# A two-layer transformer trunk: paired softmax reciprocals, one modulation row on TensorE, and the residual weighted ahead of the output projection

## The chip, the cores and the metric

The kernel runs on one core of one Trainium2 chip. The core has TensorE (PE; its weight loads are listed apart as PEld), VectorE (DVE), ScalarE (ACT), GpSimd (POOL) and SyncE (SP), which here only issues DMAs. The metric is the device time of one execution in microseconds (us), as the median of several runs. The profile is that of one execution.

## The reference

Two layers act on 1024 tokens of width 1024, in float32. In short:

```python
mod = silu(c) @ w_ada[l] + b_ada[l]
shift, scale, gate = split(mod, 3)
h = x * (1 + scale) + shift
# one projection h @ w_in feeds three groups of heads and a gate:
#   6 latent heads (MLA, rotary part, RMS-normed latents), causal softmax
#   6 dilated heads: three dilated windows mixed by their softmax sums, ALiBi
#   4 sparse heads: an indexer scores all keys, the best 256 are attended, ALiBi
y = concat(latent, dilated, sparse) * silu(p_gate)
x = layer_norm(ALPHA * x + (1 + gate) * (y @ w_out[l]), ln_g[l], ln_b[l])
```

`ALPHA` is the fourth root of 4. `c` is one row of 1024 values, so `mod` is a product of one row with a 1024 x 3072 matrix.

## The kernel before

All tensors are cut into tiles of 128 partitions. Products keep float32 accuracy by splitting each operand into a rounded part `hi` and a rest `lo` and adding three products (`three`). For a weight, `split_w` (L188) loads a raw tile on SP, ScalarE makes `hi` (L192) and by default GpSimd makes `lo = raw - hi` (L193). The modulated input is held as eight blocks `HA[k]`, one for each 128 columns of the model width, each with a `hi` and a `lo` tile of 128 x 1024.

**The order of the work.** The program is written in a plain order, but a planner orders it at build time: it simulates the engines with its own cost estimates and puts instructions of different heads, stages and layers beside each other wherever their inputs and buffers allow, with preference to what comes first in the code. The order of each engine and of SP's queue is fixed before the run; semaphores carry what one engine must wait for from another.

**Stages.** `begin` makes the first layer's `h` and the dilated heads' values. Then, in each layer, `indexer` projects and scores for the sparse heads (L436 adds up a score row from PSUM), `heads_bc` runs the dilated heads (B), `select` finds each query's 256th best score bit by bit on VectorE and ScalarE (L462, L480, L485), `heads_bc` runs the sparse heads (C), `mla` the latent heads (A), and `out_proj` the output projection, residual and LayerNorm. `later` adds up the remaining modulation rows on VectorE (L256), between the indexer's jobs of layer 0.

**begin.** For each k, `part_ada(k)` loads two 128 x 1024 weight tiles (e = 0 and e = 1, the scale and the shift of block k). For each, eight VectorE instructions (L913, L915) multiply 128 x 128 pieces by a column of `cs`, the SiLU of c, and add them up in `part`; a one-column matmul with a vector of ones (L916) sums over the partitions into a column of the PSUM tile `o_ps`. L918 adds the bias into `mod0`. `part_h(k)` loads the transposed input (L922), splits a weight tile for every second k, applies scale and shift on ScalarE (L927), rounds (L928) and subtracts (L929; GpSimd, VectorE for k = 7). `part_vb(k)` runs 21 matmuls of 392 columns (L899), three products into each of seven PSUM banks. `LEAD` = 3 says by how many blocks `part_ada` runs ahead of `part_h` in the code.

**Softmax.** `attend` (L296) goes through a head in four groups of two query blocks. For each block, matmuls write the scores to PSUM; VectorE adds bias and takes the extremum (L283, or L286 and L289 for the latent heads); ScalarE takes the exponential and its sum `den` (L291); VectorE inverts the sum (L292); GpSimd, and VectorE where the table `NE` says so, multiplies the block by it (L293). Then TensorE transposes pieces of both blocks (L315), ScalarE and VectorE split them (L318, L319), and TensorE multiplies with the values (L327). L331 to L334 combine and gate. There are 16 heads in each layer, so 128 groups and 256 blocks in all.

**out_proj.** For each of eight token tiles and each half of 512 columns, 24 matmuls run into one PSUM bank. VectorE multiplies by the gate (L856), adds ALPHA times the residual (L857), and takes statistics (L858, L860, L862). GpSimd takes the power -0.5 (L863). In layer 1, L867 and L868 normalise and apply gain and bias, and the result is stored (L869). In layer 0 the stored `x1` is the normalised value without gain and bias, so in layer 1 GpSimd first applies layer 0's gain and bias to each loaded tile (L843, L844), in place. The ring `XR` holds one buffer for these loads in layer 0 and two in layer 1.

Of the kernel before, what the change touches and what calls it, by code (L numbers as in the profile page):

```python
# [21 lines left out]
P = 128  # L22
# [19 lines left out]
NX = 6  # L42
LEAD = 3

# [17 lines left out]

NPL = 2

EARLY = (2,2)
# [41 lines left out]
def trunk(ctx: ExitStack, tc: tile.TileContext, a, out):  # L107
# [32 lines left out]
    o_ps = ps_o.tile([P, 2, 256], F32, name="O")  # L140

    ident = sb.tile([P, P], F32, name="ident")
    causb = sb.tile([P, 512], BF16, name="causb")
# [37 lines left out]
    g1_d = [dr.tile([1, 1024], F32, name=f"g1_d{i}") for i in range(DEPTH)]  # L181
    x1_d = [dr.tile([P, 1024], F32, name=f"x1_d{i}") for i in range(NB)]


# [87 lines left out]

    def softmax(qb, banks, bias, scale, slots, ne):


        n = (qb + 1) * P
        p = slots[qb] if slots else PR.whole() if n > 512 else PR.next()
        mx = small.tile([P, 2], F32, name="mx")
        den = small.tile([P, 1], F32, name="den")
        for i, (o, w) in enumerate(pieces(n)):  # L280
            first, m = mx[:, 0:1] if i else -LOW, mx[:, i:i + 1]
            if bias is not None:
                dve.tensor_tensor_reduce(p[:, o:o + w], banks[i][:, :w], bias(qb, o, w), -scale, first,  # L283
                                         OP.add, OP.min, accum_out=m)
            elif o + w == n:
                dve.tensor_tensor_reduce(p[:, o:o + w], banks[i][:, :w], causb[:, 512 - w:], scale[:, qb:qb + 1], first,  # L286
                                         OP.add, OP.min, accum_out=m)
            else:
                dve.tensor_scalar(p[:, o:o + w], banks[i][:, :w], scale[:, qb:qb + 1], first, OP.mult, OP.min,  # L289
                                  accum_out=m)  # L290
        act.activation(p[:, :n], p[:, :n], AF.Exp, bias=m, scale=-1.0, accum_out=den)  # L291
        dve.reciprocal(den, den)  # L292
        (dve if ne[qb] else pool).tensor_scalar(p[:, :n], p[:, :n], den, 0.5, OP.mult, OP.mult)  # L293
        return lambda kb: p[:, kb * P:kb * P + P]

    def attend(lab, passes, vt, bias, scale, y, r0, order=(0, 1, 2, 3), done=None, slots=None):  # L296

        for g in order:
            p = []
            for qb in (2 * g, 2 * g + 1):  # L300
                n = (qb + 1) * P
                banks = []
                for o, w in pieces(n):
                    ps = ps_s.tile([P, 512], F32, name="S")
                    chain(ps[:, :w], [(q[:, qb * P:(qb + 1) * P], k[:, o:o + w]) for q, k in passes])
                    banks.append(ps)
                p.append(softmax(qb, banks, bias, scale, slots, NE[layer[0]]["ABC".index(lab[0])]))
            o = o_ps[:, g % 2, :]
            for kp in range(g + 1):
                t = ps_t.tile([P, 512], F32, name="T")  # L310
                full = kp < g
                at = [(0, 0, 0), (0, 1, 128), (1, 1, 256)] if not full else \
                     [(0, 0, 0), (0, 1, 128), (1, 0, 256), (1, 1, 384)]
                for kk, j, c in at:
                    pe.transpose(t[:, c:c + P], p[j](2 * kp + kk), ident)  # L315
                n = len(at) * P
                pt = PT.next().rearrange("p (a b) -> p a b", a=2)
                act.activation(pt[:, 0, :n], t[:, :n], AF.Copy)  # L318
                dve.tensor_tensor(pt[:, 1, :n], t[:, :n], bc(pt[:, 0, :n]), OP.subtract)  # L319
                for kk in range(2):  # L320
                    kb = 2 * kp + kk
                    if kk == 1 and not full:
                        oc, pc = slice(128, 256), slice(256, 384)
                    else:
                        oc, pc = slice(0, 256), slice(kk * 256, kk * 256 + 256)
                    for e in range(2):
                        pe.matmul(o[:, oc], lhsT=vt(kb), rhs=pt[:, e, pc], start=(kb == 0 and e == 0),  # L327
                                  stop=(kb == 2 * g + 1 and e == 1), skip_group_check=True)
# [350 lines left out]
    def mla(l, values):  # L679
# [79 lines left out]

        q, y = {}, {}  # L760
        keys(0)
# [6 lines left out]
        for h in range(6):  # L768
# [19 lines left out]
            for i in range(NQ[l][h], NQ[l][h + 1]):  # L788
                if i < 5:
                    query(i)  # L790

    def out_proj(l):
# [11 lines left out]
        f = G.n % 2 ^ 1  # L804
        XR = Ring([AC[0]] + ([G.tiles[f]] if last else []))
        at = {3: (Vs[4], Vs[5]), 4: (Vs[0], Vs[1]), 5: W.tiles[0:2], 6: W.tiles[2:4],
# [14 lines left out]
        sp.dma_start(g1, g1_d[l].to_broadcast([P, 1024]))  # L821
        lgb = []
        if last:
            for t, src in zip([fresh("pt0", F32), fresh("pt1", F32), PR3[2], PR3[1]],
                              (a["ln_g"][0], a["ln_b"][0], a["ln_g"][1], a["ln_b"][1])):
                sp.dma_start(t, src.to_broadcast([P, 1024]))
                lgb.append(t)
        else:
# [9 lines left out]
        for tb in TBO:  # L838
            tok = slice(tb * P, (tb + 1) * P)
            xr = XR.next()  # L840
            sp.dma_start(xr, x1_d[tb] if last else a["x"][tb])
            if last:
                pool.tensor_tensor(xr, xr, lgb[0], OP.mult)  # L843
                pool.tensor_tensor(xr, xr, lgb[1], OP.add)  # L844
            r = X.next()
# [18 lines left out]
            if last:  # L864
                for n in range(2):
                    cols = slice(n * 512, (n + 1) * 512)
                    dve.scalar_tensor_tensor(r[:, cols], r[:, cols], mv[:, 0:1], lgb[2][:, cols], OP.subtract, OP.mult)  # L867
                    dve.scalar_tensor_tensor(r[:, cols], r[:, cols], rs, lgb[3][:, cols], OP.mult, OP.add)  # L868
                    sp.dma_start(out[tb][:, cols], r[:, cols])  # L869
# [13 lines left out]
    def begin():  # L883
# [18 lines left out]
        def part_ada(k):  # L902
            for e in range(2):
                w = ring.next()
                sp.dma_start(w, a["w_ad0"][e, k])
                if k == 0 and e:
                    sp.dma_start(bcol, a["b_ad0"])
                    dve.tensor_scalar(bcol[:, 0, :], bcol[:, 0, :], 1.0, None, OP.add)
                part = cols[:, (2 * k + e) % 8, :]
                for c in range(8):  # L910
# [3 lines left out]
                    else:  # L914
                        dve.scalar_tensor_tensor(part, wc, cs[:, c:c + 1], part, OP.mult, OP.add)  # L915
                pe.matmul(o_ps[:, 0, 2 * k + e:2 * k + e + 1], lhsT=part, rhs=ones, start=True, stop=True,  # L916
                          skip_group_check=True)
            dve.tensor_tensor(mod0[:, :, k], o_ps[:, 0, 2 * k:2 * k + 2], bcol[:, :, k], OP.add)  # L918

        def part_h(k):  # L920
            x = xs.next()
            sp.dma_start(x, a["xt"][k])  # L922
            if k % 2 == 0:
                hi, lo = split_w(a["wvb"][0, k // 2], 784, ring=QK, raws=raws)
                for j in range(2):
                    wv.append((hi[:, j * 392:(j + 1) * 392], lo[:, j * 392:(j + 1) * 392]))
            act.activation(x, x, AF.Identity, scale=mod0[:, 0, k:k + 1], bias=mod0[:, 1, k:k + 1])  # L927
            act.activation(HA[k][0], x, AF.Copy)  # L928
            (dve if k == 7 else pool).tensor_tensor(HA[k][1], x, bc(HA[k][0]), OP.subtract)  # L929

        for k in range(-LEAD, 9):
            if 0 <= k + LEAD < 8:
                part_ada(k + LEAD)
            if 0 <= k < 8:
                part_h(k)
            if k > 0:
# [130 lines left out]
```

## Time and profile before

| | |
|---|---|
| median of 3 runs | 1795.9 us |
| lowest, highest run | 1790.45, 1797.68 us |
| the profiled execution's own time | 1791.37 us |
| its span, first to last instruction | 1789.5 us |
| mean granted TensorE clock | 0.978 |

In a profile row, `L915 DVE` is line 915 of the kernel on VectorE; `out<-in` names the tiles; `x56` is a count; in groups, the figures behind the bar are busy us in all and mean ns of one, and then the idle time of the engine just before them with what ended most of it. A row of one line gives min/median/max ns, and the first and the last start in us. In the timeline a row begins with start and duration in us. A row of the table of waits says who waited for whom, the us in total, the times, and the longest. Matmuls are pipelined and their ends are modelled, so a busy TensorE is not at its peak.

### The profile page before, as it was taken

To read this page: it belongs to the slowest core of one execution; us is meant where nothing else is said; L and a number is where in the kernel's file an instruction comes from. 1 tells how busy PE (TensorE), PEld (TensorE's weight loads), DVE (VectorE), ACT (ScalarE), POOL (GpSimd) and SP (SyncE) were. 2 spreads that over 40 slices of the span, in tenths; PEclk is the share of its full clock that TensorE was granted. 3 is DMA by queue.
4 is the path that set the end of the run, shared out by engine and by line. 5 is a ranking of instruction groups with operands and counts; after the bars stand their busy time and mean duration, and the time that the engine had idled before them with its cause. 6 is when DMAs were issued, how large, how long until landed. Compare 5 with 4: busy or idle time off the path is not lost. (4 is left out here: it accounts for less than half of the span.)

```text
span 1789.5 us, 26735 instructions
## 1 busy us (share of the span) xinstructions
PE 1662.4 (93%) x9080; PEld 1440.0 (80%) x9080; DVE 1396.6 (78%) x3266; ACT 1022.0 (57%) x2010; POOL 697.8 (39%) x625
## 2 busy tenths in 40 slices
PE   4899899999998999989999989999999999998993
PEld 4778688888896888877899978888789788987882
DVE  8889788889588678886763678888948866788589
ACT  3244499895544666674113649998544367767500
POOL 3421134233434355463322113323343345666274
PEclk9899999999999999999999999999999999999997
DMA  9465113233212521222332212242220244122232
GB/s 345 147 220 189 48 55 92 78 119 102 75 36 62 212 92 57 84 68 92 110 130 51 71 59 56 75 142 83 74 92 20 67 171 141 45 76 91 71 106 94
DMA packets 55364, 178.93 MB, mean 100 GB/s; under 512 B 7606, under 2 KB 8630, under 8 KB 54716
## 3 DMA queue, kind: packets, MB, share of 16 engines
q1 hardware_dynamic: 50812, 147.86, 24.7%
q0 software_dynamic: 4416, 29.36, 5.7%
q8 instruction: 72, 1.18, 0.3%
q14 instruction: 64, 0.52, 0.1%
HBM read 129.74 MB, written 34.87 MB: 92 GB/s over the span
## 5 line engine op out<-in xcount | busy, mean ns | idle before, releaser
L199 PE MATMUL pj<-h,w 128*128 128x512 f32 (+1 forms) x3408 | 831.1, 391 | 13.9 <-DVE qk L233 5.4
L199 PEld LDWEIGHTS pj<-h,w 128*128 128x128 f32 x3408 | 632.2, 191 | 131.6 <-issue 12.6
L193 POOL TENSOR_TENSOR w<-wr,w 128x1024 fp32r<-128x1024 f32 (+2 forms) x86 | 192.9, 2244 | 284.4 <-ACT w L192 262.7
L199 PE MATMUL S<-qk,qk 128*128 128x512 f32 (+2 forms) x1104 | 281.9, 360 | 11.0 <-DVE mx L283 4.6
L293 POOL TENSOR_SCALAR pr<-pr,den 128x896 f32<-128x896 f32 (+7 forms) x180 | 139.0, 776 | 257.3 <-DVE den L292 214.0
L318 ACT ACTIVATE pt<-T 128x512 fp32r<-128x512 f32 (+1 forms) x320 | 172.1, 551 | 112.6 <-PE T L315 56.3
L319 DVE TENSOR_TENSOR pt<-T,pt 128x512 fp32r<-128x512 f32 (+1 forms) x320 | 199.6, 633 | 43.1 <-ACT pt L318 38.9
L327 PE MATMUL O<-pt,v 128*128 128x256 f32 (+1 forms) x1280 | 213.0, 286 | 7.3 <-DVE pt L319 4.2
L199 PEld LDWEIGHTS S<-qk,qk 128*128 128x128 f32 x1104 | 185.2, 191 | 36.7 <-DVE mx L283 8.7
L480 ACT ACTIVATE scr<-acc,U 128x768 uint8<-128x768 f32 x186 | 193.2, 1039 | 33.6 <-DVE U L476 18.1
L327 PEld LDWEIGHTS O<-pt,v 128*128 128x128 f32 x1280 | 185.6, 191 | 24.0 <-DVE pt L319 6.8
L334 POOL TENSOR_TENSOR g<-g,osum 64x256 f32<-64x256 f32 x128 | 98.6, 770 | 224.0 <-DVE osum L332 222.3
L291 ACT ACTIVATE pr<-pr,mx 128x384 f32<-128x384 f32 (+7 forms) x188 | 145.6, 775 | 54.7 <-DVE mx L283 36.4
L315 PE MATMUL T<-ident,pr 128*128 128x128 f32 x852 | 144.7, 278 | 9.7 <-POOL pr L293 5.1
L462 DVE TENSOR_SCALAR_CACHE_REDUCE scr<-acc,U 128x384 uint8<-128x384 f32 x186 | 138.4, 744 | 3.8
L192 ACT ACTIVATE w<-wr 128x1024 fp32r<-128x1024 f32 (+2 forms) x86 | 83.8, 976 | 65.0 <-PE pj L199 62.3
L315 PEld LDWEIGHTS T<-ident,pr 128*128 128x128 f32 x852 | 101.4, 141 | 21.0 <-POOL pr L293 6.5
L199 PE MATMUL pj<-w,h 128*128 128x256 f32 (+2 forms) x672 | 107.0, 300 | 1.4 <-DMA h<-cq_d 1.2
L199 PEld LDWEIGHTS pj<-w,h 128*128 128x128 f32 x672 | 91.7, 190 | 6.3 <-DMA h<-cq_d 1.4
L331 ACT ACTIVATE osum<-O 64x256 f32<-64x256 f32 x128 | 48.6, 380 | 58.5 <-PE O L327 55.3
L436 DVE SCALAR_TENSOR_TENSOR acc<-S,wi,acc 128x512 f32<-128x512 f32 (+1 forms) x84 | 56.2, 679 | 30.6 <-ACT S L431 30.3
L332 DVE TENSOR_TENSOR osum<-O,osum 64x256 f32<-64x256 f32 x128 | 53.4, 417 | 26.2 <-ACT osum L331 22.6
(277 smaller groups left out, 2565.2 us busy)
## 6 DMA issues: line engine op xcount, KB each, us to landing
wr<-in_wt_dram SPq DMA_DIRECT2D x62, 512.0 KB, 3.6
cq_d<-rw SPq DMA_DIRECT2D x64, 256.0 KB, 2.0
h<-cq_d POOLq DMA_DIRECT2D x4, 4096.0 KB, 20.2
qk<-qk POOLq DMA_DIRECT2D x48, 256.0 KB, 2.9
pt<-in_w_ada_dram SPq DMA_DIRECT2D x22, 512.0 KB, 4.0
wr<-in_w_out_dram SPq DMA_DIRECT2D x16, 512.0 KB, 3.5
bi<-in_bias_dram SPq DMA_DIRECT2D x14, 512.0 KB, 4.1
bi<-in_w_ada_dram SPq DMA_DIRECT2D x10, 512.0 KB, 4.5
```

Source lines behind the costliest of these rows:

```text
L192: act.activation(hi[:, :n], raw[:, :n], AF.Copy)
L193: (lo_eng or pool).tensor_tensor(lo[:, :n], raw[:, :n], bc(hi[:, :n]), OP.subtract)
L199: pe.matmul(ps, lhsT=l, rhs=r, start=(i == 0), stop=(i == len(items) - 1))
L291: act.activation(p[:, :n], p[:, :n], AF.Exp, bias=m, scale=-1.0, accum_out=den)
L293: (dve if ne[qb] else pool).tensor_scalar(p[:, :n], p[:, :n], den, 0.5, OP.mult, OP.mult)
L315: pe.transpose(t[:, c:c + P], p[j](2 * kp + kk), ident)
L318: act.activation(pt[:, 0, :n], t[:, :n], AF.Copy)
L319: dve.tensor_tensor(pt[:, 1, :n], t[:, :n], bc(pt[:, 0, :n]), OP.subtract)
L327: pe.matmul(o[:, oc], lhsT=vt(kb), rhs=pt[:, e, pc], start=(kb == 0 and e == 0), stop=(kb == 2 * g + 1 and e == 1), skip_group_check=True)
L334: pool.tensor_tensor(yc, yc, s[r0:r0 + 64], OP.mult)
L462: dve.tensor_scalar(scr8[:, :IDX_LEN[b]], scores(b), s, None, op, OP.add, accum_out=dst[:, b:b + 1])
L480: act.activation(scr[:, :IDX_LEN[b]], scores(b), AF.Sign, bias=U[:, b:b + 1].bitcast(F32), accum_out=cnt[:, b:b + 1])
```

## The change

Four things are changed.

1. Softmax: the two blocks of a group put their sums into the two columns of one `den` tile; one reciprocal inverts both after the second block's exponential, and then both blocks are scaled, by the same engines as before.
2. begin: for e = 0 the eight 128 x 128 pieces go straight to TensorE as eight one-column matmuls that add up in PSUM; VectorE's chain stays for e = 1. The `lo` subtractions of the weights of `part_h` and of all `HA[k]` are VectorE's. `LEAD` is 1, and `part_h(k)` stands ahead of `part_ada(k + 1)`.
3. Residual: a new function `residual(i)` loads an x1 tile into a new tile `RES`, applies layer 0's gain and bias on GpSimd, and stores it in a new DRAM tile `xw_d`. It is called in layer 1's `mla`, two tiles behind each of heads 0 to 3 (`NRES`). `out_proj` of layer 1 loads `xw_d` and no longer has L843 and L844. `XR` gets `RES` as one more buffer in both layers. Gain and bias live in new tiles `LNG` and `LNB`.
4. The SBUF space for descriptors of GpSimd's own DMAs is set to 4096 bytes a partition; the three new tiles take 12 KB a partition.

```diff
-LEAD = 3
+LEAD = 1
+NRES = ((0,0,0,0,0,0),(2,2,2,2,0,0))
+    RES, LNG, LNB = [sb.tile([P, 1024], F32, name=n) for n in ("res", "lng", "lnb")]
...
-    def softmax(qb, banks, bias, scale, slots, ne):
+    def softmax(qb, banks, bias, scale, slots, den):
...
-        den = small.tile([P, 1], F32, name="den")
...
         act.activation(p[:, :n], p[:, :n], AF.Exp, bias=m, scale=-1.0, accum_out=den)
-        dve.reciprocal(den, den)
-        (dve if ne[qb] else pool).tensor_scalar(p[:, :n], p[:, :n], den, 0.5, OP.mult, OP.mult)
-        return lambda kb: p[:, kb * P:kb * P + P]
+        return p[:, :n]
...
         for g in order:
             p = []
+            den = small.tile([P, 2], F32, name="den")
             for qb in (2 * g, 2 * g + 1):
...
-                p.append(softmax(qb, banks, bias, scale, slots, NE[layer[0]]["ABC".index(lab[0])]))
+                p.append(softmax(qb, banks, bias, scale, slots, den[:, qb % 2:qb % 2 + 1]))
+            dve.reciprocal(den, den)
+            ne = NE[layer[0]]["ABC".index(lab[0])]
+            for j in range(2):
+                (dve if ne[2 * g + j] else pool).tensor_scalar(p[j], p[j], den[:, j:j + 1], 0.5, OP.mult, OP.mult)
...
             for i in range(NQ[l][h], NQ[l][h + 1]):
                 if i < 5:
                     query(i)
+            for _ in range(NRES[l][h]):
+                residual(rest.pop(0))
+
+    def residual(i):
+        if i == 0:
+            sp.dma_start(LNG, a["ln_g"][0].to_broadcast([P, 1024]))
+            sp.dma_start(LNB, a["ln_b"][0].to_broadcast([P, 1024]))
+        tb = TBO[i]
+        sp.dma_start(RES, x1_d[tb])
+        pool.tensor_tensor(RES, RES, LNG, OP.mult)
+        pool.tensor_tensor(RES, RES, LNB, OP.add)
+        sp.dma_start(xw_d[tb], RES)
...
-        XR = Ring([AC[0]] + ([G.tiles[f]] if last else []))
+        XR = Ring([AC[0], RES] + ([G.tiles[f]] if last else []))
...
-        lgb = []
         if last:
-            for t, src in zip([fresh("pt0", F32), fresh("pt1", F32), PR3[2], PR3[1]],
-                              (a["ln_g"][0], a["ln_b"][0], a["ln_g"][1], a["ln_b"][1])):
-                sp.dma_start(t, src.to_broadcast([P, 1024]))
-                lgb.append(t)
+            sp.dma_start(LNG, a["ln_g"][l].to_broadcast([P, 1024]))
+            sp.dma_start(LNB, a["ln_b"][l].to_broadcast([P, 1024]))
...
-            sp.dma_start(xr, x1_d[tb] if last else a["x"][tb])
-            if last:
-                pool.tensor_tensor(xr, xr, lgb[0], OP.mult)
-                pool.tensor_tensor(xr, xr, lgb[1], OP.add)
+            sp.dma_start(xr, xw_d[tb] if last else a["x"][tb])
...
-                part = cols[:, (2 * k + e) % 8, :]
+                to = o_ps[:, 0, 2 * k + e:2 * k + e + 1]
+                if e == 0:
+                    for c in range(8):
+                        pe.matmul(to, lhsT=w[:, c * P:(c + 1) * P], rhs=cs[:, c:c + 1], start=(c == 0), stop=(c == 7),
+                                  skip_group_check=True)
+                    continue
+                part = cols[:, k % 8, :]
...
-                hi, lo = split_w(a["wvb"][0, k // 2], 784, ring=QK, raws=raws)
+                hi, lo = split_w(a["wvb"][0, k // 2], 784, ring=QK, lo_eng=dve, raws=raws)
...
-            (dve if k == 7 else pool).tensor_tensor(HA[k][1], x, bc(HA[k][0]), OP.subtract)
+            dve.tensor_tensor(HA[k][1], x, bc(HA[k][0]), OP.subtract)
 
         for k in range(-LEAD, 9):
+            if 0 <= k < 8:
+                part_h(k)
             if 0 <= k + LEAD < 8:
                 part_ada(k + LEAD)
-            if 0 <= k < 8:
-                part_h(k)
             if k > 0:
                 part_vb(k - 1)
...
-    nc = bacc.Bacc("TRN2", target_bir_lowering=False, num_devices=1)
+    nc = bacc.Bacc("TRN2", target_bir_lowering=False, num_devices=1, dynamic_dma_scratch_size=4096)
```

More of the change, by code (lines that the diff above doesn't have):

```diff
@@ L182, in trunk @@
     x1_d = [dr.tile([P, 1024], F32, name=f"x1_d{i}") for i in range(NB)]
+    xw_d = [dr.tile([P, 1024], F32, name=f"xw_d{i}") for i in range(NB)]
     def bc(t):
@@ L314, in attend @@
                 for kk, j, c in at:
-                    pe.transpose(t[:, c:c + P], p[j](2 * kp + kk), ident)
+                    pe.transpose(t[:, c:c + P], p[j][:, (2 * kp + kk) * P:(2 * kp + kk + 1) * P], ident)
                 n = len(at) * P
@@ L758, in query @@
             project(wh, wl, 6, CA, evac)
-        q, y = {}, {}
+        q, y, rest = {}, {}, list(range(NB))
         keys(0)
@@ L866, in out_proj @@
                     cols = slice(n * 512, (n + 1) * 512)
-                    dve.scalar_tensor_tensor(r[:, cols], r[:, cols], mv[:, 0:1], lgb[2][:, cols], OP.subtract, OP.mult)
-                    dve.scalar_tensor_tensor(r[:, cols], r[:, cols], rs, lgb[3][:, cols], OP.mult, OP.add)
+                    dve.scalar_tensor_tensor(r[:, cols], r[:, cols], mv[:, 0:1], LNG[:, cols], OP.subtract, OP.mult)
+                    dve.scalar_tensor_tensor(r[:, cols], r[:, cols], rs, LNB[:, cols], OP.mult, OP.add)
                     sp.dma_start(out[tb][:, cols], r[:, cols])
@@ L915, in part_ada @@
                         dve.scalar_tensor_tensor(part, wc, cs[:, c:c + 1], part, OP.mult, OP.add)
-                pe.matmul(o_ps[:, 0, 2 * k + e:2 * k + e + 1], lhsT=part, rhs=ones, start=True, stop=True,
-                          skip_group_check=True)
+                pe.matmul(to, lhsT=part, rhs=ones, start=True, stop=True, skip_group_check=True)
             dve.tensor_tensor(mod0[:, :, k], o_ps[:, 0, 2 * k:2 * k + 2], bcol[:, :, k], OP.add)
```

## The prediction

> **What bounds the kernel now.** I read the page's head first, then busy time by stretches, then the groups and waits of the two stretches where TensorE is not full. The head:
>
> ```profile
> span 1789.5 us, 26735 instructions
> PE 1662.4 (93%) x9080; PEld 1440.0 (80%) x9080; DVE 1396.6 (78%) x3266; ACT 1022.0 (57%) x2010; POOL 697.8 (39%) x625
> ```
>
> TensorE is busy for 93% of the span, so most of the program is out of reach of an edit that does not touch its matmuls. The 127 us left lie mostly at the two ends. At the start (columns: stretch, busy time and instructions of PE, PEld, DVE, ACT, POOL, granted clock, DMA share, GB/s):
>
> ```profile
> 0.00:20.00 20.00, 2.35 (x8) 2.00 (x8) 15.12 (x66) 4.54 (x5) 1.20 (x5) 1.00 0.91 337
> 20.00:40.00 20.00, 14.11 (x69) 12.94 (x70) 19.69 (x43) 5.94 (x6) 10.78 (x5) 1.00 1.00 365
> 40.00:60.00 20.00, 15.20 (x74) 14.55 (x74) 19.75 (x37) 8.41 (x9) 15.25 (x6) 0.83 0.35 122
> 60.00:80.00 20.00, 16.43 (x81) 15.42 (x81) 14.59 (x27) 8.60 (x13) 6.20 (x3) 0.91 0.48 157
> ...
> PE O L916 <- DVE g L915: 25.7, 7, 9.4
> ...
> L915 DVE SCALAR_TENSOR_TENSOR g<-acc,cs,g 128x128 f32<-128x128 f32 x56 | 25.4, 483 | 0.5
> L915 DVE SCALAR_TENSOR_TENSOR g<-bi,cs,g 128x128 f32<-128x128 f32 x28 | 14.7, 548 | 0.1
> L915 DVE SCALAR_TENSOR_TENSOR g<-pr,cs,g 128x128 f32<-128x128 f32 x21 | 8.5, 431 | 0.0
> L929 POOL TENSOR_TENSOR h<-v,h 128x1024 fp32r<-128x1024 f32 x7 | 19.3, 2755 | 10.3 <-ACT h L928 10.3
> ...
> 7.23 1.66 DVE L915 SCALAR_TENSOR_TENSOR g<-acc,cs,g 128x128 f32<-128x128 f32 x6
> ...
> 73.49 0.52 PE L899 MATMUL T<-qk,h 128*128 128x392 f32 x2
> ```
>
> The opening ends with its last L899 matmul at 74.0 us. From 20 to 60 us VectorE is full (19.69 and 19.75 of 20), and TensorE waits 25.7 us for the modulation sums of L915. Six of these take 1.66 us when nothing disturbs them, 0.28 us each, but the 105 shown took 48.6 us where 105 x 0.28 is 29: VectorE lost some 19 us while GpSimd ran its subtractions. The DMA is full only up to 40 us.
>
> At the end, from the timeline and two groups:
>
> ```profile
> 1711.65 2.39 POOL L843 TENSOR_TENSOR g<-g,pt 128x1024 f32<-128x1024 f32 x1
> 1714.12 2.73 POOL L844 TENSOR_TENSOR g<-g,pt 128x1024 f32<-128x1024 f32 x1
> ...
> 1711.71 5.68 DVE L857 SCALAR_TENSOR_TENSOR acc<-acc 128x512 f32<-128x512 f32 x2
> ...
> L857 DVE SCALAR_TENSOR_TENSOR acc<-acc x20: 677/968/2883, 847.4 to 1773.6; 128x512 f32<-128x512 f32 x20
> ...
> L868 DVE SCALAR_TENSOR_TENSOR acc<-acc,rs,pr 128x512 f32<-128x512 f32 x12 | 17.4, 1481 | 0.0
> ...
> 1754.87 1.66 PE L199 MATMUL pj<-v,h 128*128 128x512 f32 x6 [2.26 <-DVE acc L856]
> 1760.21 0.39 PE L199 MATMUL pj<-rw,h 128*128 128x512 f32 x1
> ...
> 1780.72 0.69 DVE L856 TENSOR_TENSOR pr<-pj,bi 128x512 f32<-128x512 f32 x1
> 1785.30 1.00 SPq L869 DMA_DIRECT2D out_dram<-pr  x2
> ```
>
> Two L857 start just after L843 and end (1717.39) just after L844 (1716.85): 5.68 us for what takes 0.68 each alone. A VectorE instruction that reads two SBUF tensors stands still while GpSimd works. VectorE therefore falls behind TensorE, holds it up once (2.26 us) and goes on for 25 us after the last matmul (1760.6).
>
> **The opening, step by step.** Removed: the e=0 half of the VectorE chain, 64 instructions. Added on VectorE: seven more lo subtractions of h (1024 wide) and four of the weights (784 wide). The nearest row for such a two-input operation is L256; the ACT steps and the TensorE prices are here too:
>
> ```profile
> L256 DVE SCALAR_TENSOR_TENSOR g<-pt,cs,g x22: 1273/1285/2955, 70.6 to 168.5; 128x1024 f32<-128x1024 f32 x22
> L927 ACT ACTIVATE v<-v,mod x8: 1226/1240/1244, 16.3 to 64.7; 128x1024 f32<-128x1024 f32 x8
> L928 ACT ACTIVATE h<-v x8: 1039/1048/1058, 18.8 to 66.8; 128x1024 fp32r<-128x1024 f32 x8
> ...
> 150.59 1.62 PE L261 MATMUL O<-ones,g 128*128 128x1 f32 x14
> ...
> 54.27 1.18 PE L899 MATMUL S<-qk,h 128*128 128x392 f32 x3
> 55.25 0.86 PE L899 MATMUL T<-qk,h 128*128 128x392 f32 x2
> ...
> 58.35 0.70 PE L899 MATMUL S<-qk,h 128*128 128x392 f32 x3
> 58.89 0.52 PE L899 MATMUL T<-qk,h 128*128 128x392 f32 x2
> ```
>
> VectorE afterwards: 64 x 0.28 = 17.9 us, 8 x 1.27 = 10.2, 4 x 1.27 x 784/1024 = 3.9, together 32 us or 4.0 for each of the eight k. GpSimd has nothing left there, so nothing stretches it. TensorE for each k: 21 L899 at (58.89 - 58.35)/3 = 0.18 us make 3.8, and nine one-column matmuls at 1.62/14 = 0.12 make 1.0, in all 4.8. ACT: 1.24 + 1.05 and half a weight copy, under 3. The loads: 24 tiles of 0.524 MB and four of 0.40, 14.2 MB, of which 40 us carry 14.0 at the 337 and 365 GB/s shown, 5.1 us for each k. So the DMA becomes the bound. LEAD = 1 puts x of block k ahead of the modulation weights of k+1, which changes the order of these loads on SP, not their sum. The last block lands near 41 us; ACT (2.3) and 21 matmuls (3.8) end at 47, with the semaphores at 48. That is the low bound. The high one is TensorE at half speed throughout: (55.25 - 54.27)/3 = 0.33 us a matmul, 7.9 for each k, 63 for eight, some 66 with the first load. I take 53, nearer the floor since three engines lie under the DMA's 5.1, with 5 us for handovers: **-21 us**, between -26 and -8. What follows (indexer projections, the later modulation rows) moves up by as much, since it starts from h.
>
> The trace shows two speeds of the same matmul, 0.33 and 0.18 us. The Trainium skill ("TensorE: Matmul & The Clock Gate", What's actually happening) puts this down to an activity window of about 3.4 us: half clock after an idle window, full clock after a busy one. By that rule gaps of 0.3 us between blocks would leave the clock high; but the VectorE chain of each k could widen them, and then up to 3.4 us of each k would go at half speed, an estimate of 14 us in all. I keep that as a rival.
>
> **The reciprocals.** 128 of 256 one-column instructions go; the other 128 get two columns.
>
> ```profile
> L292 DVE RECIPROCAL den<-den x256: 132/159/166, 231.5 to 1671.5; 128x1 f32<-128x1 f32 x128
> ...
> L293 POOL TENSOR_SCALAR pr<-pr,den 128x896 f32<-128x896 f32 (+7 forms) x180 | 139.0, 776 | 257.3 <-DVE den L292 214.0
> ...
> PE T L315 <- POOL pr L293: 5.1, 5, 2.0
> ```
>
> At most 128 x 0.16 = 20 us of VectorE are saved, in stretches where TensorE is already full. In exchange the first block's scale waits for the second block's exponential, and then both scales run one after the other: 0.78 us later for the second, for the transposes queued behind it on TensorE and for the rest of GpSimd's queue (L334). Over 128 groups that is 99 us if nothing hid it. But the transposes of a group need both blocks already now, and TensorE was held by L293 five times for 5.1 us in all: score matmuls of later blocks and projections cover it. I take **-1 us**, between -8 and +12 for the uncovered cases; the full 99 is a rival below.
>
> **The residual.** Two GpSimd operations for each of eight tiles leave the tail, with the four L826 loads. New are eight loads of x1, eight stores of 512 KB, and two loads of the gains, on SP; then a reload of the second pair of gains. The code puts them behind heads 0 to 3 of layer 1's latent attention, but the planner issues what is ready:
>
> ```profile
> L872 SPq DMA_DIRECT2D x_d<-pr x2: 319/322/326, 870.0 to 919.1; - x2
> L832 DVE TENSOR_TENSOR lnc<-lnc,scale_n x1: 158/158/158, 160.1 to 160.1; 128x8 f32<-128x8 f32 x1
> ...
> 960.00:1000.00 40.00, 40.00 (x225) 38.96 (x224) 23.79 (x40) 21.91 (x42) 12.13 (x8) 1.00 0.30 76
> 1000.00:1040.00 40.00, 40.00 (x193) 34.68 (x192) 24.15 (x40) 23.88 (x45) 5.66 (x3) 1.00 0.21 74
> 1550.00:1590.00 40.00, 39.62 (x232) 34.70 (x231) 30.10 (x69) 24.07 (x47) 21.85 (x21) 1.00 0.16 47
> ...
> L436 DVE SCALAR_TENSOR_TENSOR acc<-S,wi,acc x84: 469/743/752, 125.4 to 1065.5; 128x512 f32<-128x512 f32 x56, 128x256 f32<-128x256 f32 x14, 128x384 f32<-128x384 f32 x14
> ```
>
> L832 belongs to layer 0's output projection (L857 there begins at 847.4 us) and ran at 160 us, as soon as its input was there. The residual's inputs, the x1 tiles, are all on their way to memory at 919 us. I expect it in layer 1's indexer, from about 920: 16 x 2.4 us (L843's undisturbed 2.39) = 38 us of GpSimd in a stretch where it is busy 12 and 6 of 40. The two-SBUF-input trouble is small there, since L436 reads PSUM and never exceeds 0.75 us. One buffer (RES) chains load, two operations and store tile by tile; on SP each load waits for the store before it, and the weight loads (L191) queued behind wait too, which the second weight buffer covers. Price: the weight splits of GpSimd, each up to 4.8 us later, for which TensorE might wait: **+2 us**, from 0 to +38 (all on the path; what is left of GpSimd where the code has it, 18 of 40, is the nearest row for that).
>
> **The tail.** With L843 and L844 gone, VectorE needs ten operations of about 0.7 us and the small ones, 7.5 us a tile, against 48 matmuls at (1760.6 - 1754.87)/24 = 0.24 us, 11.5: it keeps up, and TensorE sets the end. TensorE ends 2.26 earlier, at 1758.3. From the last L856 to the span's end pass 1789.5 - 1780.72 = 8.8 us. So the end comes at 1767: **-21 us** (22.4, rounded for a last tile that queues a little). The low bound is only what L868's group lost, 12 x (1.48 - 0.7) = 9. The third XR buffer and ready tiles cover the loads; without that cover the final chain would be later by a landing.
>
> The smaller descriptor space of GpSimd's DMAs makes room for the three new tiles. The largest DMA of that queue:
>
> ```profile
> h<-cq_d POOLq DMA_DIRECT2D x4, 4096.0 KB, 20.2
> ```
>
> If its descriptors no longer fitted at once it would come in portions, at worst one more landing of 20 us in each layer; if they fit, nothing. No row shows the limit. I take nothing, since the planner starts this load while other heads run, and leave the 20 to the range.
>
> **Sum.** -21 - 1 + 2 - 21 = -41. The profiled execution took 1791.4 us for its span of 1789.5, 4.5 under the median of the runs (1795.9). 1791.4 - 41 = 1750; allowing for part of that spread I predict **1753**.
>
> **Rivals.**
> - Residual where the code has it. GpSimd, at 22 of 40 in the heads' stretch, gets 38 us more over four heads and delays their scales. Half of it on the path: 1753 + 18 = 1771. For it: these heads' priority is the code's order. Against: L832.
> - Opening at half clock, or VectorE's chain still late: it ends at 66, 13 later: 1766.
> - The tail is not cured: L857 was long for its loads, not for GpSimd. Then 21 us stay: 1774. Against: L843 itself had started, so its load had landed.
> - Slower: pairing the reciprocals decides in the sparse and dilated heads. In 80 of the 128 groups the scale comes 0.78 us late on the path: +62, so 1815. For it: GpSimd's idle time before L293 ends with L292 (214 us), so every later reciprocal moves the scale. It outweighs the gains from 41/0.78 = 53 groups on. Against: the 5.1 us above.
>
> **How the numbers follow.** The forecast gets 0.62 (its own range 1738 to 1768), the residual in place 0.14, the opening 0.13, the uncured tail 0.06, pairing 0.05. The range 1735 to 1780 takes in the first four nearly whole. About 0.5% (9 us) is what the measurement can tell from no change. Faster than 1787: all but pairing and two rivals together, 0.92; within, 0.04; slower than 1805, 0.04.
>
> **What would show it.** Right: L899 ends near 53; no GpSimd work before that; L857 and L868 near 0.7 us each in the tail, and the span's end 9 us behind the last matmul; the weighting near 920 to 1050; TensorE's wait for L293 still under 10 us. Wrong: weighting after 1500 with GpSimd over 30 of 40; matmuls of 0.33 us all through the opening; or TensorE losing tens of us to the scales.

## The result, and the profile after

| | before | changed |
|---|---|---|
| median | 1796.7 us | 1764.4 us |
| lowest, highest | 1790.5, 1797.7 us | 1762.2, 1768.2 us |
| profiled span | 1789.5 us | 1760.5 us |
| opening's last L899 (L913 after) starts | 73.7 us | 61.4 us |
| from there to the latent heads' last score operation | 1595.5 us | 1598.9 us |
| from there to the end (tail) | 120.3 us | 100.2 us |

The ratio is 0.983, with a 95% interval of 0.980 to 0.986: 32 us faster, in the range (1735 to 1780), 11 us above the forecast of 1753. The head of the page of the changed kernel:

```profile
span 1760.5 us, 26767 instructions
PE 1677.6 (95%) x9192; PEld 1454.5 (83%) x9192; DVE 1341.7 (76%) x3085; ACT 1020.4 (58%) x2010; POOL 667.6 (38%) x614
```

TensorE has more to do (15 us), VectorE 55 us less. Changed kernel, busy time by stretches of the opening (columns as in the prediction):

```profile
0.00:20.00 20.00, 12.49 (x52) 12.35 (x53) 11.65 (x40) 5.50 (x6) 0.19 (x4) 1.00 0.90 341
20.00:40.00 20.00, 19.55 (x136) 19.38 (x134) 15.59 (x36) 11.88 (x11) 0.86 (x1) 1.00 1.04 404
40.00:60.00 20.00, 19.93 (x121) 19.85 (x120) 12.73 (x24) 7.96 (x7) 4.00 (x2) 0.91 0.73 263
```

VectorE is no longer the full engine (15.6 of 20). TensorE is, and the DMA too up to 40 us. Its timeline there, with the new e = 0 matmuls (L927) between the blocks of L913:

```profile
11.64 3.58 PE L927 MATMUL O<-cs,acc 128*128 128x1 f32 x16 [1.59 <-DVE mod L939]
15.08 1.00 PE L913 MATMUL pj<-qk,h 128*128 128x392 f32 x2
...
20.63 0.28 PE L938 MATMUL O<-ones,g 128*128 128x1 f32 x2
...
26.12 1.84 PE L927 MATMUL O<-cs,g 128*128 128x1 f32 x16
...
61.24 0.52 PE L913 MATMUL T<-qk,h 128*128 128x392 f32 x2
```

The code issues eight L927 for each k; the rows count 16. A float32 matmul with one moving column leaves two records here, 1.84/16 = 0.115 us each, or 0.23 us for each matmul of the code. The first row's 3.58 us is a slower speed, though the granted clock of that stretch reads 1.00: up to about 19 us one L913 takes 0.33 us too, and 0.18 later. L938, one matmul for each k, shows two as well.

The softmax, groups of lines (columns: busy us, mean ns | idle time before them and what ended it). L334 is the value matmul (L327 before), L322 the transposes, L314 GpSimd's scale, L311 the two-column reciprocal:

```profile
L334 PE MATMUL O<-pt,v 128*128 128x256 f32 (+1 forms) x1280 | 214.0, 287 | 21.6 <-DVE pt L326 9.8 <-DVE osum L339 5.5 <-ACT pt L325 4.8
L322 PE MATMUL T<-ident,pr 128*128 128x128 f32 x852 | 141.9, 279 | 2.4 <-POOL pr L314 1.8 <-DVE pt L326 0.5
L314 POOL TENSOR_SCALAR pr<-pr,den 128x896 f32<-128x896 f32 (+7 forms) x180 | 141.3, 796 | 214.2 <-DVE den L311 158.1 <-PE pj L204 21.1 <-PE T L322 13.3
L311 DVE RECIPROCAL den<-den 128x2 f32<-128x2 f32 x128 | 20.5, 160 | 15.5 <-ACT pr L295 9.0 <-ACT acc L295 3.7 <-ACT bi L295 1.5
```

The same value matmuls, the transposes and the reciprocals in the kernel before:

```profile
L327 PE MATMUL O<-pt,v 128*128 128x256 f32 (+1 forms) x1280 | 213.0, 286 | 7.3 <-DVE pt L319 4.2 <-DVE osum L332 1.5 <-ACT pt L318 1.1
L315 PE MATMUL T<-ident,pr 128*128 128x128 f32 x852 | 144.7, 278 | 9.7 <-POOL pr L293 5.1 <-DVE pt L319 4.4
L292 DVE RECIPROCAL den<-den 128x1 f32<-128x1 f32 x256 | 39.0, 158 | 26.1 <-ACT pr L291 18.9 <-ACT acc L291 4.1 <-ACT bi L291 1.5
```

The reciprocals cost half as much (20.5 us for 39.0), but TensorE's idle time ahead of the value matmuls went from 7.3 to 21.6 us. Ahead of the transposes it fell from 9.7 to 2.4, so a part of it has only moved; the two together went from 17.0 to 24.0. The residual (L808 multiplies, L809 adds; min/median/max ns, first and last start), and the stretches in which it runs:

```profile
L808 POOL TENSOR_TENSOR res<-res,lng x8: 2375/2396/2404, 908.1 to 990.8; 128x1024 f32<-128x1024 f32 x8
...
900.00:950.00 50.00, 49.02 (x275) 46.60 (x274) 21.98 (x37) 8.91 (x17) 30.51 (x16) 1.00 0.38 137
950.00:1000.00 50.00, 49.66 (x273) 47.31 (x272) 28.82 (x49) 26.93 (x53) 33.37 (x16) 1.00 0.52 171
```

It runs in layer 1's indexer, at 908 to 996 us, and TensorE stays full (49.0 and 49.7 of 50). The tail (L871 and L882 are L857 and L868 of before), with the last matmul and the last store:

```profile
L871 DVE SCALAR_TENSOR_TENSOR acc<-g,acc x4: 683/688/693, 1708.4 to 1731.1; 128x512 f32<-128x512 f32 x4
L882 DVE SCALAR_TENSOR_TENSOR acc<-acc,rs,lnb x12: 699/744/747, 1705.2 to 1745.7; 128x512 f32<-128x512 f32 x12
...
1751.67 0.39 PE L204 MATMUL pj<-rw,h 128*128 128x512 f32 x1
...
1756.68 0.99 SPq L883 DMA_DIRECT2D out_dram<-pr  x2
```

L868's group took 1481 ns in the mean; L882's takes 739. The span ends 8.4 us behind the last matmul.

### The profile page after: what moved, and what is told of

Same layout as the page of the kernel before. It is cut to its first block, busy times and chain, and to the rows that moved or that the text cites. A ratio compares the mean times of both kernels' runs of the same rounds, so it can differ in the third digit from the quotient of the medians.

```text
span 1760.5 us, 26767 instructions
## 1 busy us (share of the span) xinstructions
PE 1677.6 (95%) x9192; PEld 1454.5 (83%) x9192; DVE 1341.7 (76%) x3085; ACT 1020.4 (58%) x2010; POOL 667.6 (38%) x614
## 4 chain that ended last, share of the span: by engine, by line
PE 64%; DVE 18%; ACT 9%; issue 5%; DMA 3%; POOL 1%; SPq 0%; DVEq 0%; ACTq 0%; POOLq 0%
PE pj L204 36%; PE S L204 12%; PE O L334 6%; PE T L322 5%; ACT scr L487 4%; DVE scr L469 2%; DVE pt L326 1%; DVE pr L538 1%; DVE acc L443 1%; ACT pt L325 1%; DVE pr L287 1%; ACT pr L295 1%; PE T L204 1%; DMA h<-cq_d 1%; DVE scr L543 1%
## 5 line engine op out<-in xcount | busy, mean ns | idle before, releaser
L334 PE MATMUL O<-pt,v 128*128 128x256 f32 (+1 forms) x1280 | 214.0, 287 | 21.6 <-DVE pt L326 9.8
L314 POOL TENSOR_SCALAR pr<-pr,den 128x896 f32<-128x896 f32 (+7 forms) x180 | 141.3, 796 | 214.2 <-DVE den L311 158.1
L334 PEld LDWEIGHTS O<-pt,v 128*128 128x128 f32 x1280 | 185.8, 191 | 42.8 <-DVE pt L326 14.7
L322 PE MATMUL T<-ident,pr 128*128 128x128 f32 x852 | 141.9, 279 | 2.4 <-POOL pr L314 1.8
L197 ACT ACTIVATE w<-wr 128x1024 fp32r<-128x1024 f32 (+2 forms) x86 | 83.9, 977 | 73.7 <-PE pj L204 65.1
L322 PEld LDWEIGHTS T<-ident,pr 128*128 128x128 f32 x852 | 101.9, 143 | 12.9 <-POOL pr L314 3.0
## 6 DMA issues: line engine op xcount, KB each, us to landing
h<-cq_d POOLq DMA_DIRECT2D x4, 4096.0 KB, 19.7
```

The lines of the kernel that those rows point to most:

```text
L197: act.activation(hi[:, :n], raw[:, :n], AF.Copy)
L314: (dve if ne[2 * g + j] else pool).tensor_scalar(p[j], p[j], den[:, j:j + 1], 0.5, OP.mult, OP.mult)
L322: pe.transpose(t[:, c:c + P], p[j][:, (2 * kp + kk) * P:(2 * kp + kk + 1) * P], ident)
```

## The experiments

The table cuts each profiled span at two marks: the start of the opening's last weight-times-h matmul, and the latent heads' last score operation on VectorE. The last column is worked out from all 256 exponentials and scales of a trace: the mean time from the end of an exponential to the start of its block's scale. Medians are of 4 to 13 executions, of one for e11 and e12.

| kernel | median us | ratio (95%) | opening | middle | tail | exponential to scale |
|---|---|---|---|---|---|---|
| before | 1794 to 1797 | 1 | 73.7 | 1595.5 | 120.3 | 1.26 |
| changed | 1764.4 | 0.983 (0.980 to 0.986) | 61.4 | 1598.9 | 100.2 | 3.95 |
| e1 residual alone | 1765.8 | 0.985 (0.983 to 0.988) | 77.1 | 1591.2 | 97.1 | |
| e2 opening alone | 1783.8 | 0.995 (0.994 to 0.997) | 61.9 | 1600.3 | 120.3 | |
| e3 reciprocals alone | 1812.4 | 1.011 (1.008 to 1.015) | 73.5 | 1608.8 | 123.6 | 3.99 |
| e4 all but reciprocals | 1751.7 | 0.977 (0.975 to 0.980) | 65.9 | 1589.6 | 97.2 | 1.28 |
| e5 half the opening | 1761.1 | 0.980 (0.978 to 0.982) | 72.0 | 1591.1 | 97.1 | |
| e6 late gains | 1762.9 | 0.982 (0.979 to 0.984) | 64.1 | 1601.9 | 97.2 | |
| e7 two reciprocals behind both | 1748.6 | 0.974 (0.972 to 0.976) | 63.7 | 1584.4 | 99.9 | 1.23 |
| e8 paired in latent heads | 1767.0 | 0.984 (0.981 to 0.986) | 61.4 | 1599.8 | 100.1 | 2.09 |
| e9 scales bound to both | 1788.1 | 0.996 (0.994 to 0.997) | 63.7 | 1622.0 | 100.6 | 4.76 |
| e10 half the matmuls | 1758.9 | 0.980 (0.978 to 0.983) | 60.1 | 1590.5 | 99.8 | |
| e11 tail reads | 1768.4 | | 61.6 | 1585.5 | 118.5 | |
| e12 tail writes | 1752.6 | | 65.8 | 1585.3 | 99.8 | |

One thing first on its precision. Every edit lets the planner find another order. The middle of the kernels that have neither paired reciprocals nor an edit meant for it (before, e1, e2, e4, e5, e7, e10) lies between 1584 and 1600 us, 1592 in the mean. So a difference of 5 us in the middle between two kernels says little about the edit. The middles of the changed kernel (1598.9) and of e8 (1599.8) lie within that range; those of e3 (1608.8) and e9 (1622.0) lie above it, and above e6's 1601.9.

### The parts one by one: e1 to e4

e1 has the residual's edit alone, e2 the opening's, e3 the reciprocals':

```diff
+            dve.reciprocal(den, den)
+            ne = NE[layer[0]]["ABC".index(lab[0])]
+            for j in range(2):
+                (dve if ne[2 * g + j] else pool).tensor_scalar(p[j], p[j], den[:, j:j + 1], 0.5, OP.mult, OP.mult)
```

and e4 is the changed kernel with these lines back inside `softmax`, one block at a time.

> The kernel before with the residual part alone (residual(), RES, LNG, LNB, the third XR buffer, the smaller descriptor space). Theory: the tail's loss comes from GpSimd's L843 and L844 alone, and the weighting is free where the planner puts it: -20 us against the kernel before (the tail from the last exponential to the end shrinks from 118 us to 98), opening unchanged at 74 us. Rival (the tail owes its gain to something else in the change, or the weighting costs what it saves): 0 to -8 us.

> The kernel before with the opening's part alone. Theory: the opening ends near 62 us as in the changed kernel or, because the loads of RES, LNG and LNB are not there to be put ahead of the last blocks' loads, some 4 us earlier: -12 to -16 us in all, tail unchanged at 118 us. Rival (the opening's gain is given back in the indexer): -5 us or less.

> The kernel before with the paired reciprocals alone. Theory 1 (the 3 to 4 us that the changed kernel loses between opening and tail are the price of the later scales): +3 to +6 us. Theory 2 (the saved VectorE time is worth as much as the delay; the loss in the middle is the planner's new order): -2 to +2 us.

> The changed kernel with the reciprocals one by one as before. Theory 1: 3 to 6 us faster than the changed kernel (-35 to -38 against the kernel before). Theory 2: the same as the changed kernel within 2 us (-30 to -34).

Measured: e1 about 29 us faster, 23 of them in the tail. e2 about 11 us faster, all of it in the opening. e3 is 18 us slower, and e4 13 us faster than the changed kernel. So the residual pays its 20 us and more, the opening about half of what I forecast, and the reciprocals cost time. The groups of value matmuls, scales and transposes in e3 (L329, L309 and L317 there), and of value matmuls and transposes in e4 (L332 and L320):

```profile
L329 PE MATMUL O<-pt,v 128*128 128x256 f32 (+1 forms) x1280 | 214.8, 286 | 23.2 <-DVE pt L321 10.8 <-ACT pt L320 5.7 <-DVE osum L334 5.2
L309 POOL TENSOR_SCALAR pr<-pr,den 128x896 f32<-128x896 f32 (+7 forms) x180 | 140.9, 795 | 222.0 <-DVE den L306 157.5 <-PE T L317 26.2 <-DVE U L490 17.5
L317 PE MATMUL T<-ident,pr 128*128 128x128 f32 x852 | 141.7, 278 | 4.1 <-DVE pt L321 2.0 <-POOL pr L309 1.9
```

```profile
L332 PE MATMUL O<-pt,v 128*128 128x256 f32 (+1 forms) x1280 | 212.9, 286 | 9.8 <-DVE pt L324 4.2 <-ACT pt L323 3.2 <-DVE osum L337 2.0
L320 PE MATMUL T<-ident,pr 128*128 128x128 f32 x852 | 145.6, 279 | 6.2 <-POOL pr L298 3.1 <-DVE pt L324 3.0
```

TensorE's idle time before the value matmuls follows the pairing: 7.3 us before, 9.8 in e4, 23.2 in e3, 21.6 in the changed kernel. With the transposes' added it is 17.0, 16.0, 27.3 and 24.0 us. In the ten kernels without pairing this sum lies between 13.3 and 17.0, so here the paired ones stand clear of the scatter. It accounts for 8 us of the 13 and 10 of the 18; where the rest is lost isn't shown.

### Is it the delay? e7, e9, e8

e7 is the changed kernel with two one-column reciprocals in place of the paired one; e9 puts a copy of both sums ahead of them:

```diff
-            dve.reciprocal(den, den)
+            rs = small.tile([P, 2], F32, name="rs")
+            dve.tensor_copy(rs, den)
+            for j in range(2):
+                dve.reciprocal(rs[:, j:j + 1], rs[:, j:j + 1])
```

> The changed kernel with the order of the pairing but without its saving: both exponentials, then two one-column reciprocals, then both scales. Theory, what costs is the place of the scales (the first block's scale waits for the second block's exponential): as slow as the changed kernel, 1764 to 1772, ratio 0.983 to 0.987. Rival, what costs is the two-column instruction or the sums shared in one tile: near e4, ratio 0.977.

> The kernel of e7 (two one-column reciprocals, where the planner issued each right behind its own exponential, 0.42 us in the median, so that nothing was delayed), with a two-column copy of the sums ahead of both reciprocals: now neither block's scale can start before the second block's exponential, and nothing is saved (128 small copies more). Theory, the delay of the first block's scale is what pairing costs: 10 to 20 us slower than e7, 1760 to 1770, ratio 0.98 to 0.985, and TensorE waits for transposed weights again (value matmuls' gaps near 6 us in the sparse and dilated stage of each layer). Rival, the planner merely found a worse order when instructions were taken out: near e7, 1749 to 1753, ratio 0.975.

e7 was not the test that I meant. In its trace a reciprocal starts 0.43 us behind its own exponential in the median, for the first blocks as for the second, and the scale 1.23 us behind in the mean: the planner moved the first block's work ahead of the second exponential, whatever the order of the code. e7 shows only that sums in two columns of one tile cost nothing that could be told from the scatter. It is the fastest kernel, 47 us under the one before and 16 under the changed one.

e9 does impose the wait, and the scale then starts 4.76 us behind the exponential. It is 39 us slower than e7, which is far outside the scatter of the orders, and more than I expected (10 to 20). Its value matmuls and its copies:

```profile
L337 PE MATMUL O<-pt,v 128*128 128x256 f32 (+1 forms) x1280 | 218.5, 290 | 14.9 <-DVE pt L329 6.2 <-DVE osum L342 6.0 <-ACT pt L328 2.5
L325 PE MATMUL T<-ident,pr 128*128 128x128 f32 x852 | 144.1, 278 | 10.2 <-DVE pt L329 5.6 <-POOL pr L317 4.5
...
L312 DVE COPY rs<-den x128: 136/169/2218, 221.4 to 1688.5; 128x2 f32<-128x2 f32 x128
```

The same two groups in e7, where TensorE is idle 8.9 + 5.8 = 14.7 us and not 14.9 + 10.2 = 25.1:

```profile
L335 PE MATMUL O<-pt,v 128*128 128x256 f32 (+1 forms) x1280 | 213.6, 286 | 8.9 <-DVE pt L327 4.5 <-DVE osum L340 1.8 <-DVE lastc L542 1.2
L323 PE MATMUL T<-ident,pr 128*128 128x128 f32 x852 | 143.2, 277 | 5.8 <-DVE pt L327 2.7 <-POOL pr L315 2.6
```

These two groups hold 10 us of the 39. In the whole middle TensorE is idle 79.4 us in e9 and 58.6 in e7, 20.8 more, and the same matmuls keep it busy for 1542.6 us and not 1525.8, 16.8 more, at a mean granted clock of 0.98 and not 0.99. The 128 copies are some 128 x 0.17 = 22 us of VectorE, an engine that is busy for three quarters of the span; what share of the 39 us they have was not tried apart.

e8 keeps the pairing in the latent heads (A) alone:

```diff
+                if lab[0] != "A":
+                    dve.reciprocal(d, d)
+                    (dve if ne[qb] else pool).tensor_scalar(p[-1], p[-1], d, 0.5, OP.mult, OP.mult)
```

> The changed kernel with the pairing kept in the latent heads alone; the sparse and dilated heads have a reciprocal and a scale for each block again. Theory, the cost lies where TensorE waits for weights of a group with little other work ahead, which is the sparse and dilated heads: near e4, 1752 to 1756, ratio 0.977 to 0.979. Rival, the latent heads carry their share (64 of 128 groups): half of the loss stays, 1758, ratio 0.980.

Neither held. The latent heads are 6 of 16, so 48 of the 128 groups are paired and not the 64 of the expectation, and yet it is as slow as the changed kernel. Beside e4, its layer-0 latent heads take 5 us longer and the stretch from layer 1's first latent group to the end 6 us longer; the sparse and dilated stages, each from its start to the start of the next, differ by about 1 us or less. That points at the latent heads, which I took to have slack, but such differences are no larger than the scatter, and TensorE's idle time ahead of the transposes and value matmuls is 18.6 us, 2.6 over e4's. Where e8 loses its time, and why pairing the rest as well adds nothing, is not shown by any run here.

### What bounds the opening: e5, e10, e6

e5 is e4 with the scale row of odd k back on VectorE; e10 is e7 with half of the one-column matmuls:

```diff
-                if e == 0:
+                if e == 0 and k % 2 == 0:
```

```diff
-                    for c in range(8):
+                    for c in range(4):
```

> The kernel of e4 (no paired reciprocals), with the scale row of the odd blocks k put back on VectorE; TensorE keeps it for the even k. Theory, TensorE bounds the opening: the 64 one-column matmuls of one k run as 128 in all, 1.84 us per k, so TensorE needs 47 us from its first matmul; with half of them gone it needs 8 x 0.92 = 7 us less, while VectorE gets 4 x 2.24 = 9 us more, which lies beside. The opening ends near 56 to 58 us instead of 61.7 (65.9 in e4), and the time falls by 4 to 7 us against e4: 1745 to 1748, ratio near 0.973. Rival, the loads bound it, or the hoisted loads of the gains and of the first residual tile: no change, 61 to 66 and 1752. Rival, VectorE bounds it: it gets later, by up to 9 us.

> The kernel of e7, where four of the eight one-column matmuls of each output block's scale are left out (half of that sum is missing, so the modulation is another one). Theory, TensorE bounds the opening, because these float32 matmuls run as two passes each (16 records for 8 matmuls, 1.84 us): 0.92 us less for each of eight k, so the opening ends near 56 us instead of 63.7 if the clock stays full, and the time falls by 5 to 8 us to 1742. If the clock falls to a half for a stretch, up to 5 us of that are lost; the period of a k at full clock tells: 4.9 us against 5.8. Rival, the loads or VectorE bound it at nearly the same level: the period stays above 5.5 us and the end at 61 to 64.

In e5 the second rival came true: the opening ends 6 us later than in e4. Its stretches, and TensorE's wait for ScalarE's h, which comes behind VectorE's sums:

```profile
20.00:40.00 20.00, 19.59 (x108) 19.51 (x107) 19.66 (x50) 9.72 (x10) 3.47 (x1) 0.83 1.02 387
40.00:60.00 20.00, 15.19 (x84) 15.03 (x84) 14.87 (x35) 7.85 (x7) 2.47 (x1) 0.87 0.72 272
60.00:80.00 20.00, 17.39 (x76) 16.57 (x75) 13.36 (x25) 5.58 (x10) 0.00 (x0) 0.79 0.35 114
...
PE pj L911 <- ACT h L947: 12.2, 4, 4.7
```

VectorE is full again (19.66 of 20), TensorE has gaps, and its granted clock is 0.87 and then 0.79 in the two stretches behind. In e10, L928 takes 0.95 us where it took 1.84, as it should, but the opening ends only 3.6 us before e7's and 1.3 before the changed kernel's. Timelines of TensorE, VectorE and SP, and the table of DMA issues:

```profile
38.75 0.95 PE L928 MATMUL O<-cs,acc 128*128 128x1 f32 x8
...
48.58 0.16 DVE L940 TENSOR_TENSOR mod<-O,bcol 128x2 f32<-128x2 f32 x1 [2.82 <-PE O L939]
...
48.80 1.05 PE L928 MATMUL O<-cs,bi 128*128 128x1 f32 x8 [0.26 <-DVE mod L940]
...
51.16 0.62 PE L914 MATMUL pj<-qk,h 128*128 128x392 f32 x2 [0.51 <-ACT h L950]
...
36.70 0.38 SPq L920 DMA_DIRECT2D bi<-in_w_ad_dram  x1
...
bi<-in_w_ad_dram SPq DMA_DIRECT2D x4, 512.0 KB, 9.4
```

The last modulation weights are issued at 36.70 us and, with 9.4 us to landing, arrive near 46. TensorE takes up the last block's (`bi`) at 48.80, so they are there in time, and from 20 to 62 us none of its waits is for a DMA. It waits 4.0 us there (0.5 in e7), mostly for VectorE's `mod` and ScalarE's h; VectorE for its part waits 5.6 us for TensorE's L939, 2.82 of them in the row at 48.58, and two blocks' matmuls still follow. Behind the first L914 six of the new groups are half as long, which is some 5 us, and 3.5 of these come back as such waits. So TensorE bounds the opening of the changed kernel, and its exchange with VectorE and ScalarE is so close behind that halving the new matmuls wins 1 to 4 us, not 7. The theory holds for the bound and falls for its lead. The whole kernel is 10 us slower than e7 in the median, with 6 us more in the middle. The period of a k went to no clear figure, since the clock fell twice.

e6 keeps three loads that the planner had put among these (the gains, the shifts and the first residual tile) out of the opening:

```diff
+            for t in (RES, LNG, LNB):
+                dve.tensor_copy(t[:, 0:1], rk[:, 0:1])
```

> The kernel of e4, where small copies keep the first loads of the gains, the shifts and the first residual tile from being issued before layer 0's selection is done; they no longer stand among the opening's loads. Theory, TensorE bounds the opening: it ends as in e4 or the changed kernel (61 to 66 us), and the time is within 2 us of e4. Rival, these three loads (1.5 MB, 4 us of the transfer rate) hold up the last weights and x: the opening ends about 4 us earlier and the time falls by 4 us.

The opening ends at 64.1 us, as in e7 (63.7), so these loads did not hold it up. The 11 us that e6 loses to e4 lie behind it: 5 us more up to the first exponential and 6 in layer 0's heads and selection. Which instruction pays there is open.

The opening with the same code ended anywhere from 61.4 to 65.9 us (changed, e2, e4, e6 to e9, e11, e12). The granted clock puts these nine in order: up to the mark its mean is 0.97 where the opening ends at 61.4 to 61.9, 0.95 at 63.7 to 64.1, and 0.90 at 65.8 and 65.9. A stretch of e4, and a row of its new matmuls there:

```profile
24.00:36.00 12.00, 12.00 (x44) 12.00 (x44) 6.94 (x16) 4.68 (x5) 0.00 (x0) 0.50 1.04 399
...
28.43 3.41 PE L925 MATMUL O<-cs,g 128*128 128x1 f32 x16
```

In the changed kernel:

```profile
24.00:36.00 12.00, 12.00 (x82) 12.00 (x82) 10.41 (x26) 6.13 (x7) 0.00 (x0) 1.00 1.04 400
```

For 12 us the clock is at half in one execution and full in the other, behind a gap of about the same length (0.25 us in e4, 0.26 in the changed kernel). What decides between the two no run here shows.

### The tail: e11, e12

e7, with two operations of GpSimd for each tile of layer 1's projection whose result nobody uses:

```diff
+                for _ in range(2):
+                    pool.tensor_tensor(dmy, xr, LNG, OP.mult)
```

and in e12 `pool.memset(dmy, 0.0)` in place of the product.

> The kernel of e7 with 16 products on GpSimd added to layer 1's output projection, two for each tile; they read the residual tile and the gains and write a buffer that nobody reads or waits for. Theory, VectorE's operations on two SBUF tensors stand still while GpSimd reads SBUF: the normalization's operations stretch from 0.7 us to 2 us and more, and the tail (last exponential to end, 98 us) grows by 10 to 20 us though no instruction waits for GpSimd. Rival, the old tail was long because VectorE waited for GpSimd's results: no change, within 3 us.

> As e11, with memsets of the same tile in place of the products: GpSimd writes SBUF and reads nothing. Theory, only reads stop VectorE: its operations stay near 0.7 us and the tail within 3 us of e7. Rival, any work of GpSimd stops it: longer in proportion to GpSimd's busy time.

The tail takes 118.5 us in e11, 99.8 in e12 and 99.9 in e7. Groups of the tail in e11, with a row of TensorE's waits, and then in e12:

```profile
L887 DVE SCALAR_TENSOR_TENSOR acc<-acc,rs,lnb 128x512 f32<-128x512 f32 x12 | 26.2, 2232 | 0.0
L863 POOL TENSOR_TENSOR pt<-acc,lng 128x1024 f32<-128x1024 f32 x6 | 15.9, 2654 | 1.5 <-PE O L335 1.3
...
PE pj L204 <- DVE acc L875: 4.6, 2, 3.9
```

```profile
L863 POOL MEMSET pt<- 128x1024 f32 x16 | 15.3, 954 | 1.9 <-PE O L335 1.3
L887 DVE SCALAR_TENSOR_TENSOR acc<-acc,rs,lnb 128x512 f32<-128x512 f32 x12 | 8.4, 743 | 0.5 <-POOL rs L882 0.5
```

With products that nobody waits for, L887 takes three times as long (2232 ns for 743) and the tail is as long as that of the kernel before (120.3). With memsets nothing changes. Their time is shorter (15.3 us for about 42), but four of e12's sixteen L887 do run beside a memset and take 745 ns, the other twelve 744; in e11 the ten beside a product take 2744 and the other six 743. The Trainium skill ("SBUF — State Buffer", Who interferes with whom) has VectorE's operations with two SBUF inputs contend with a GpSimd operation that reads SBUF and not with one that only writes. Both runs agree.

## Why the prediction was right, and where it was wrong

- **The tail, -21:** right in size and cause. Measured -20.1 (120.3 to 100.2). The span ends 8.4 us behind the last matmul, 9 forecast; e11 brings the loss back with products that nobody waits for.
- **The residual, +2:** right. It ran at 908 to 996 us (920 to 1050 forecast), and TensorE stayed full. The rival "where the code has it" did not occur. Whether it cost 2 us can't be told: e1's middle is 4 us shorter than before, which is within the scatter. The smaller descriptor space, taken at nothing, cost nothing that shows: the largest DMA of that queue lands after 19.7 us, 20.2 before.
- **The opening, -21:** measured -12.3, inside its bounds. The step that failed is "nine one-column matmuls at 1.62/14 = 0.12 make 1.0": the 14 records of that row were seven matmuls. The term is 1.84 + 0.23 = 2.1 us for each k, TensorE's sum 5.9 and not 4.8, and it stands above the 5.1 of the loads, not under it. From the first L913 at 15.1 us there follow eight blocks of L913 and six of the new matmuls, 8 x 3.8 + 6 x 2.1 = 43 us; the slow speed up to about 19 us and a granted clock of 0.50 from 53.0 to 56.4 us add some 3.6, and that makes 61.7, where it ends. "The last block lands near 41 us" was some 5 us early too: the last modulation weights are issued at 36.73 us, behind five other 512 KB loads that the sum left out, and take 9.4 to land. The clock rival (half for 12 us) struck e4, not the changed kernel's profiled execution.
- **The reciprocals, -1:** wrong in sign. In pairs whose code differs in nothing else, e3 beside before and the changed kernel beside e4, the medians say +18 and +13; each pair also has two orders of the planner, so the sign holds in both and the size only to within the scatter. Two steps failed. "0.78 us later" was the price of the second scale alone; measured over both blocks, a scale starts 2.7 us later (1.26 to 3.95). The second's starts 0.6 later, but the first's 4.8 (1.2 to 6.1), since it waits for the second's exponential. And "score matmuls of later blocks and projections cover it" held for most but not all: 256 x 2.7 is 690 us of delay, and 13 to 18 us came through. I had also named the wrong sign to watch. TensorE's wait for the scale itself fell (5.1 to 1.8 us); its idle time shows one step later, ahead of the value matmuls, where it rose by 14.3 us, 7.3 of which left the transposes. My rival "pairing" had the direction right, a scale that comes late and is not covered everywhere; its price of 62 to 99 us left out most of the cover, and its place, the sparse and dilated heads alone, is not borne out by e8.
- **The sum, -41:** the profiled span gives -29.0: opening -12.3, middle +3.4, tail -20.1. The errors are +9 in the opening and +13 or so for the reciprocals in middle and tail; against them stands a middle that without the pairing is 6 us shorter than before (e4), where I forecast +2. That gain is within the scatter of the orders, and its cause stays open.
- The slower rival (1815) did not occur in the changed kernel. That e3 came near the figure (1812) is chance: it is 18 us on the kernel before, where the rival had 62 on the forecast.

## What to carry to other kernels

Price a new matmul from a row whose count of records is compared with the count in the code. When a chain per item is turned into one for two items, count the wait of the first for the second, and look for it in all the consumers further down; here two small instructions (0.16 us each) were cheaper than one. Where a planner orders the work, one small edit moves the middle by up to 8 us either way (1584 to 1600), so judge a part by pairs of kernels, and by a quantity that it acts on directly.

## What the runs showed of the hardware

- A float32 matmul with one moving column leaves two records, 1.84/8 = 0.23 us together at full clock and 3.41/8 = 0.43 at a granted clock of 0.50 (e4).
- After a gap of 0.25 us and one-column matmuls the clock stood at 0.50 for 12 us in e4 while TensorE had no idle time in its records, and at 1.00 in the changed kernel. The Trainium skill ("TensorE: Matmul & The Clock Gate", What's actually happening) has full clock return after a busy window of about 3.4 us; the 12 us of e4, busy throughout by the records, don't agree with that. What the chip counts as busy is not shown here.
- GpSimd's products of two SBUF tensors stretch VectorE's operations on two SBUF tensors (743 to 2232 ns in the mean); its memsets, which only write, don't.
- In e9's middle TensorE is idle for 20.8 us more than in e7's, and its matmuls, the same ones, also take 16.8 us more busy time, at a granted clock of 0.98 and not 0.99.
- Among nine kernels with the same code in the opening its end moved by 4.5 us with the granted clock (mean 0.97, 61.4 us; mean 0.90, 65.9 us).
